# Side jobs of a streaming encoder's input projection: roots in a row, rotated rows further apart, decay later, last part split later

## The chip, the cores and the metric

The kernel runs on one core of one Trainium2 chip. The metric is the device time of one execution in microseconds (us); lower is better. The engines of a core are TensorE (PE, with its weight loads shown as PEld), VectorE (DVE), ScalarE (ACT), GpSimd (POOL) and SyncE (SP), which only issues DMAs here; POOL issues some DMAs too.

## What is computed

One step of a one-layer encoder: a normed input is projected into [z | xBC | dt | q | k | v | gates], then come a state-space scan, differential attention, a mix and a convolutional FFN. 1024 prompt rows and 64 sample rows are treated together, 1088 columns in all. What matters here:

```python
xn = _rmsnorm(x, p['norm_mix_w'])
proj = xn @ p['w_in']
z, xbc, dt_raw, q, k, v, gate_ssm, gate_att = jnp.split(proj, ...)
...
dt = jax.nn.softplus(dt_raw + p['ssm_dt_bias'])          # the decay's steps
acum = jnp.cumsum(dtc * a_neg, axis=1)                   # per chunk, in the scan
...
y_ssm = y_ssm * jax.nn.silu(z)
...
q = _partial_rope(_rmsnorm(q.reshape(b, t, 16, 64), p['q_norm_w']), q_pos)
k = _partial_rope(_rmsnorm(k.reshape(b, t, 16, 64), p['k_norm_w']), q_pos)
k_all = jnp.concatenate([k_past, k], axis=1)             # the cached keys
```

So q and k need, beside their product, a reciprocal root over each head's 64 squares, a weight, and a rotation of the first 16 of 64 dimensions (with the layout used here, those are the first two of eight tiles of 128 rows). All is 32-bit: a float32 operand is split into a high part and a low part (the difference), and a product is three matmuls: high by high, high by low, low by high.

## The kernel before, in words

The stage in question projects q (4 pairs of tiles), k (4 pairs) and z (8 pairs), in this order, 16 pairs numbered 0 to 15 (`INPUT`). One pair is a 2 by 2 block product done with seven products instead of eight (`in_pair`): seven combinations of the weight's quadrants (on the left) times seven combinations of the normed input (on the right: b11, t2, b21, t3, t1, t4, b22), each in two halves of 272 columns. That makes 14 steps per pair, each 12 matmuls of 272 columns, numbered `at` = 0 to 13. The products gather in PSUM banks in piles: pile a holds products 0 and 2, pile b 1 and 3, pile c 4 and 6, pile d 5. A pile that is read midway (a after product 0, b after product 1, c after product 4) is read first and then added to. Piles a are read by ACT (`S.copy`, L677 and L687; the latest is kept in `seen["copy"]`), the others by DVE (L679, L681, L689; `seen["read"]`). There are seven banks in turn, and each pair takes eight.

A finished quarter of the pair goes to `done` one step later (L653): for q and k its squares (L665, L668) are summed into `squares[kind]`, for z it gets a Silu (L658); then it is stored to DRAM (L670). The row buffers `fx` (four), `fc` (three), `fp` (three), `fu` and `ss` (two) are shared by everything in this stage.

The left combinations of the next pair are made beside (`lefts_at`): loads by SP, sums by POOL (L555 to L561), a cast on ACT and a subtraction on DVE for the split (L411, L412). The right parts t3, t1, t4 and b22 had been stored to DRAM and are loaded and split (L411, L412) during pair 0 (`LATER`). The right part b12, for the gates that follow, takes t2's place once product 1 of the last pair has used it: before, load and split are both written at step (1, 1) of pair 15, `at` = 3.

Beside all this run **side jobs**, one turn per product, from the second half of pair 1 on (`take_turn`, L777). A generator in `beside` yields either a number (turns to wait before its next step) or a job (which takes its own turns; the next one comes three turns later, plus what the generator then yields). They are, in this order:

1. `steps` (L694): the decay. Softplus of dt as a series (15 DVE instructions over 288 columns, the tiles `st`, `dt`, `dtt`), cumulative sums by small matmuls, exponentials, and three pieces of decays stored to `a_sc`. Its work tile `four` is one of the two `ss` rows; the other is q's squares, and k's squares take the decay's place.
2. `cached_keys` (L864): eight jobs, each a load of 256 KB by POOL, a cast on ACT, a subtraction on DVE, and two stores.
3. `finishing("q")`, then `finishing("k")` (L796), appended when pair 3 is done. For each: sums of squares over a head (a matmul with `blk`, three pieces of 384, 384 and 320 columns), the root of each (`rstd_of`, L242: Ln, Exp and Square on ACT, two DVE instructions), then twelve jobs for the rows that aren't rotated (`part`) and four for those that are (`turned`, each 272 columns). A `turned` job loads two tiles of rows and the cosines and sines by POOL (L834, L835), and does two scalings (L842), four instructions of rotation (L846 to L849), a cast to the high part and a subtraction to the low (L768, L772), and two stores; for k also a store of the result.

The kernel is written in a framework that orders the instructions of each engine by priority (the order of writing) and by simulated readiness of the operands. `with tc.issue_after(x)` pins what is written inside behind x on x's own engine; `after("copy", "read")` pins behind the latest copy and the latest read. An activation table is loaded in front of an ACT function that the table in force does not hold; `preload_act_table_set(LN_EXP)` loads by hand the one that holds both Ln and Exp.

Of the kernel before, what the change touches and what calls it, by code (L numbers as in the profile page):

```python
# [11 lines left out]
AF = mybir.ActivationFunctionType  # L12
# [11 lines left out]
WIDE = ((0, 384), (384, 384), (768, 320))  # L24
# [66 lines left out]
def hybrid_layer(ctx: ExitStack, tc: tile.TileContext, xT, xt, prm, cst, rope, wvd, win, wbs, wba, wout, wup, wdn,  # L91
# [59 lines left out]
    def weights(block, k, m, pool=None):  # L151
# [4 lines left out]
            V.tensor_tensor(out=lo, in0=w, in1=hi, op=ALU.subtract)  # L156
        return hi, lo

    def product(ps, terms):
        n = len(terms)  # L160
        for i, (a_hi, a_lo, b_hi, b_lo) in enumerate(terms):
            PE.matmul(ps, a_hi, b_hi, start=i == 0, stop=False)  # L162
            PE.matmul(ps, a_hi, b_lo, start=False, stop=False)  # L163
            PE.matmul(ps, a_lo, b_hi, start=False, stop=i == n - 1)  # L164
# [77 lines left out]
    def rstd_of(pool, out, mean, w, tag, scale=1.0, top=384, t=None):  # L242

        t = t or [pool.tile([P, top], F32, name=f"{tag}{i}", tag=f"{tag}{i}") for i in range(2)]
        u, r = (x[: out.shape[0], :w] for x in t)
        act(u, mean, AF.Ln, bias=eps_t[: out.shape[0]], scale=scale)
        act(r, u, AF.Exp, scale=-0.5)
        act(u, r, AF.Square, scale=math.sqrt(0.5 * scale))
        V.scalar_tensor_tensor(u, mean, EPS / scale, u, ALU.add, ALU.mult)
        V.scalar_tensor_tensor(out, u, -1.5, r, ALU.add, ALU.mult)  # L250

# [216 lines left out]
    def row(tag, name, dt=F32):  # L468
        if tag in ("fa", "fs", "fu"):
            w = {"fa": KT * P, "fs": 4 * P, "fu": HT}[tag]  # L470
            return rows_l.tile([P, w], dt, name=name, tag=tag, bufs=IN_ROWS[tag])
        w = {"ss": T}.get(tag, HT)
        return rows_r.tile([P, w], dt, name=name, tag=tag, bufs=IN_ROWS[tag])
# [124 lines left out]
    FIRST_BLOCK = dict(q=B_Q, k=B_K, z=B_Z)  # L598
    LATER = {1: "t1", 3: "t4", 4: "b22"}
    squares, begun_squares = {}, set()  # L600
    seen = {}

    def blocks_of(n):
        kind, j = INPUT[n]
# [9 lines left out]
    def load_part(n, at=None):  # L614
        for s in range(2):
            hi, lo = parts[n, s] = units_of(n, s, at)
            seen["part"] = load(out=lo.bitcast(F32), in_=p_sc[n].rearrange("(k p) t -> p k t", p=P)[:, :, cols(s)])
# [11 lines left out]
    def in_pair(n):  # L629

        kind, j = INPUT[n]
        u1, u2 = row("fx" if n == 1 else "fu", "u1"), row("fu", "u2")
        banks, out = {}, {}

        def pile(key, p, s, start):
            if start:
                banks[key, s] = acc(W2[s])
            ps, w, b = banks[key, s], left[n][p], parts[PARTS[p], s]
            for k in range(4):
                c = slice(P * k, P * (k + 1))  # L640
                for i, (x, y) in enumerate(((0, 0), (0, 1), (1, 0))):
                    seen["mm"] = PE.matmul(ps, w[x][:, c], b[y][:, k], start=start and k == i == 0, stop=k == 3 and i == 2,
                                           skip_group_check=not start)
            return ps

        def to(r, c, s):

            if (r, c) not in out:
                out[r, c] = row("fp", "pre")
            a, w = O2[s], W2[s]  # L650
            return out[r, c][:, a : a + w]

        def done(r, c):  # L653
            cs = slice(HT * c, HT * (c + 1))
            t = out[r, c][:, :HT]
            f = 2 * j + r
            if kind == "z":
                act(t, t, AF.Silu)  # L658
            else:
                if kind not in squares:  # L660
                    squares[kind] = row("ss", "ss")
                ss = squares[kind][:, cs]
                if (kind, c) not in begun_squares:
                    begun_squares.add((kind, c))
                    act(ss, t, AF.Square)  # L665
                else:
                    sq = row("fc", "sq")[:, :HT]
                    act(sq, t, AF.Square)  # L668
                    V.tensor_tensor(out=ss, in0=ss, in1=sq, op=ALU.add)
            load(out={"z": z_sc, "q": q_r, "k": k_r}[kind][P * f : P * (f + 1), cs], in_=t)  # L670

        at = yield
        for _ in range(14):
            p, s = at
            us = cols(s)
            if p == 0:
                seen["copy"] = S.copy(u1[:, us], pile("a", p, s, True))  # L677
            elif p == 1:
                seen["read"] = V.tensor_tensor(out=u2[:, us], in0=pile("b", p, s, True), in1=u1[:, us], op=ALU.add)  # L679
            elif p == 3:  # L680
                seen["read"] = V.tensor_tensor(out=u1[:, us], in0=pile("b", p, s, False), in1=u1[:, us], op=ALU.add)  # L681
            else:
                r, c, key, start, u = {2: (0, 0, "a", False, None), 4: (1, 1, "c", True, u1), 5: (1, 0, "d", True, u1),
                                       6: (0, 1, "c", False, u2)}[p]
                ps = pile(key, p, s, start)
                if u is None:
                    seen["copy"] = S.copy(to(r, c, s), ps)  # L687
                else:
                    seen["read"] = V.tensor_tensor(out=to(r, c, s), in0=ps, in1=u[:, us], op=ALU.add)  # L689
                if s == 1:  # L690
                    ripe.append(lambda r=r, c=c: done(r, c))
            at = yield
# [50 lines left out]
            yield  # L743

    def one_by_one(gen):
        for _ in gen:
            yield 2

    def after(*names):
        pins = ExitStack()  # L750
        for n in names:
            pins.enter_context(tc.issue_after(seen[n].ins))
        return pins

    def job(fetch, scale, hi_of, hi_rows, lo_rows, keep=None):

# [15 lines left out]
            V.tensor_tensor(out=x.bitcast(R32), in0=x, in1=hi, op=ALU.subtract)  # L772
        load(out=lo_rows, in_=x)

    running, clock = [], [0, 0]

    def take_turn():  # L777
        for x in list(running):
            x[0] -= 1
            if x[0] <= 0:  # L780
                x[0] = next(x[1], None)
                if x[0] is None:
                    running.remove(x)
        clock[0] += 1
        if clock[0] >= clock[1]:
            new = next(beside, None)
            if new is None:
                return bool(running)
            if isinstance(new, int):
                clock[1] = clock[0] + new  # L790
            else:
                running.append([next(new), new])
                clock[1] = clock[0] + 3
        return True

    def finishing(kind):  # L796

        d, to, keep, wcol = {"q": (q_r, q_st, None, lambda j: wq8[:, j : j + 1]),
                             "k": (k_r, k_st, kT, lambda j: col(O_KN + j))}[kind]
        if kind == "q":  # L800
            yield 8
        rs = squares[kind]
        for c, w in WIDE:
            ps = stat(w)
            with tc.issue_after(seen["mm"].ins):
                PE.matmul(ps, blk, rs[:, c : c + w], start=True, stop=True)
            t = [row("fx", "n1") for _ in range(2)]
            S.copy(rs[:, c : c + w], ps)
            rstd_of(None, rs[:, c : c + w], rs[:, c : c + w], w, "qn", 1.0 / 64, t=t)
            yield 3  # L810

        def rows_at(y, r0, j, n, c, w):
            return y[r0 + P * j : r0 + P * (j + n), c : c + w].rearrange("(j p) t -> p j t", p=P)
# [45 lines left out]
            yield 1  # L859
        for c in range(0, T, QW):  # L860
            yield turned(c)
            yield 1

    def cached_keys():  # L864
        def part(j):
            def fetch():
                x = row("fx", "x")[:, :PAST]
                G.dma_start(out=x, in_=ckT[P * j : P * (j + 1), :])
                return x

            return job(fetch, None, lambda: row("fc", "xh", R32)[:, :PAST], *(c_st[D * u + P * j : D * u + P * (j + 1), :] for u in range(2)))

        for j in range(KT):
            yield part(j)
# [28 lines left out]
    for at, (p, s) in enumerate(rest):  # L903
# [7 lines left out]
                load_part("b22")  # L911
        if s == 1 and p in LATER:
            split_part(LATER[p], seen["copy"], seen["read"])
    beside = chain(one_by_one(steps()), cached_keys())
    for n in range(1, len(INPUT)):
        blocks = blocks_of(n + 1) if n + 1 < len(INPUT) else None
        u = pairs[1] if n == 1 else begun_in(n)
        for at, (p, s) in enumerate(rest if n == 1 else [(p, s) for p in range(7) for s in range(2)]):
            old, ripe = ripe, []
            u.send((p, s))  # L920
            for x in old:
                x()
            if n == 2 and at in (0, 1):
                make_left(2, 2 + at, blocks)
            lefts_at(n, at, blocks, short={3: "load", 7: 0, 9: 1} if n == 1 else None)
            take_turn()
            if n + 1 == len(INPUT) and (p, s) == (1, 1):
                load_part("b12")
                split_part("b12", seen["copy"], seen["read"])
        del left[n]  # L930
        if n == Q_DONE:
            beside = chain(beside, finishing("q"), finishing("k"))
# [1024 lines left out]
```

## Time and profile before

| | us |
|---|---|
| runs of the kernel before: median (lowest to highest of 3) | 2438.24 (2435.74 to 2441.54) |
| the profiled execution | 2441.61 |
| its span | 2439.8 |
| PE busy | 2393.0 (98%) |
| DVE busy | 1719.7 (70%) |
| ACT busy | 1222.0 (50%) |
| POOL busy | 690.9 (28%) |

The span is that of the instructions; the execution's own time has 1.8 us more around it. Busy shares are means over stages with different limits. In a timeline row the first number is the start in us from the span's start, the second the length, and the bracket at the end holds the engine's idle time just before the row and what ended it. A wait for several things is put down to the one that came last by the profile. A row "x12" is a run of 12 instructions merged.

### The profile page before, as it was taken

How to read it: one execution, taken by the hardware profiler on the slowest of the kernel's cores; microseconds unless marked ns; L12 is line 12 of the kernel's file. 1: busy time of each engine (PE TensorE's matmuls, PEld its weight loads, DVE VectorE, ACT ScalarE, POOL GpSimd, SP SyncE). 2: the span in 40 equal slices, each digit the busy share in tenths (PEclk: the TensorE clock that was granted, in tenths of full speed). 3: DMA queues.
4: the chain of work that ended last, by engine and by line, in shares of the span. 5: the costliest groups of instructions: out<-in, count | busy, mean ns of one | idle time of the engine just before them, and what ended most of it. 6: DMA issues, size and time to landing. Idle time of an engine off the chain costs nothing.

```text
span 2439.8 us, 49478 instructions
## 1 busy us (share of the span) xinstructions
PE 2393.0 (98%) x18744; PEld 2320.5 (95%) x18744; DVE 1719.7 (70%) x3090; ACT 1222.0 (50%) x2689; POOL 690.9 (28%) x757
## 2 busy tenths in 40 slices
PE   8999999999999999999999999999999999999998
PEld 8989989999999999998899999999999999999998
DVE  4676877658687786876678665756866756767765
ACT  6345465356565565657655463434533333353442
POOL 0032333201011010114344332013255554543344
PEclk9999999999999999999999999999999999999999
DMA  7855768675544444337797955764124424357976
GB/s 243 276 178 184 233 212 296 212 208 149 159 154 140 131 146 147 108 120 227 251 337 257 319 180 162 220 210 159 56 85 144 158 96 157 126 185 209 253 181 105
DMA packets 296241, 449.80 MB, mean 184 GB/s; under 512 B 36729, under 2 KB 192514, under 8 KB 296002
## 3 DMA queue, kind: packets, MB, share of 16 engines
q1 hardware_dynamic: 284962, 420.31, 52.3%
q0 software_dynamic: 11040, 26.34, 5.4%
q8 instruction: 147, 2.41, 0.4%
q14 instruction: 92, 0.75, 0.1%
HBM read 294.03 MB, written 152.50 MB: 183 GB/s over the span
## 4 chain that ended last, share of the span: by engine, by line
PE 47%; DVE 4%; DMA 2%; issue 2%; ACT 1%; POOL 0%; SPq 0%; POOLq 0%; DVEq 0%; ACTq 0%
PE mx L1599 13%; PE mx L1773 6%; PE mm L1599 5%; PE mm L162 3%; PE mm L164 3%; PE mm L163 3%; PE mx L162 3%; PE mx L164 3%; PE mx L163 3%; PE mm L1773 2%; PE yi L1288 1%; PE ye L1294 1%; PE stp L1300 1%; PE tr L1267 1%; DMA w_f<-in_wout_dram 1%
## 5 line engine op out<-in xcount | busy, mean ns | idle before, releaser
L162 PE MATMUL mm<-b,w_hi 128*128 128x272 f32 x1576 | 465.8, 296 | 0.0
L164 PE MATMUL mm<-b,w_lo 128*128 128x272 f32 x1576 | 459.3, 292 | 0.0
L163 PE MATMUL mm<-b,w_hi 128*128 128x272 f32 x1576 | 457.9, 291 | 0.0
L162 PEld LDWEIGHTS mm<-b,w_hi 128*128 128x128 f32 x1576 | 296.9, 188 | 6.2 <-issue 5.1
L163 PEld LDWEIGHTS mm<-b,w_hi 128*128 128x128 f32 x1576 | 297.1, 189 | 2.9 <-issue 2.1
L164 PEld LDWEIGHTS mm<-b,w_lo 128*128 128x128 f32 x1576 | 296.5, 188 | 0.7 <-issue 0.2
L983 DVE SCALAR_TENSOR_TENSOR cc<-pre,par,cc 128x272 f32<-128x272 f32 (+1 forms) x288 | 140.2, 491 | 15.9 <-ACT cc L981 13.0
L1599 PE MATMUL mx<-n,wh 128*128 128x272 f32 x1080 | 145.0, 290 | 1.9 <-DVE u L1626 1.0
L1599 PE MATMUL mx<-m,w_hi 128*128 128x272 f32 x752 | 144.6, 289 | 1.1 <-ACT m L411 1.1
L1599 PEld LDWEIGHTS mx<-n,wh 128*128 128x128 f32 x1080 | 139.8, 190 | 2.3 <-DVE u L1626 1.2
L971 POOL COPY pre<-pre 128x3 f32<-128x3 f32 x72 | 22.5, 312 | 417.4 <-DVE cc L985 196.3
L412 DVE TENSOR_TENSOR wh<-w_f,wh 128x512 fp32r<-128x512 f32 (+1 forms) x144 | 139.2, 967 | 1.0 <-ACT wh L411 0.9
L162 PE MATMUL mx<-b,w_hi 128*128 128x272 f32 x472 | 138.7, 294 | 0.5 <-ACT grs L1325 0.5
L164 PE MATMUL mx<-b,w_lo 128*128 128x272 f32 x472 | 137.7, 293 | 1.0 <-DVE w_lo L156 1.0
L156 DVE TENSOR_TENSOR w_lo<-w_f,w_hi 128x1024 fp32r<-128x1024 f32 (+1 forms) x82 | 102.2, 1248 | 51.3 <-ACT w_hi L155 50.3
L1107 ACT ACTIVATE p_t<-sc,mx 128x512 f32<-128x512 f32 (+6 forms) x144 | 106.1, 739 | 64.5 <-DVE mx L1098 30.3
L163 PE MATMUL mx<-b,w_hi 128*128 128x272 f32 x472 | 135.8, 288 | 0.0
L155 ACT CAST w_hi<-w_f 128x1024 fp32r<-128x1024 f32 (+1 forms) x82 | 85.8, 1048 | 71.6 <-PE mm L163 48.7
L1599 PEld LDWEIGHTS mx<-m,w_hi 128*128 128x128 f32 x752 | 118.1, 188 | 1.3 <-ACT m L411 1.3
L1608 ACT ACTIVATE cc<-pre,par 128x544 f32<-128x544 f32 (+1 forms) x44 | 37.2, 846 | 146.7 <-DVE pre L1643 146.6
L1599 PE MATMUL mx<-m,w_lo 128*128 128x272 f32 x376 | 108.3, 289 | 0.0
L1616 POOL TENSOR_TENSOR hb<-hb,cc 128x544 f32<-128x544 f32 (+2 forms) x63 | 67.0, 1078 | 132.6 <-DVE hb L1637 98.5
(461 smaller groups left out, 7084.1 us busy)
## 6 DMA issues: line engine op xcount, KB each, us to landing
w_f<-in_win_dram SPq DMA_DIRECT2D x48, 512.0 KB, 3.9
w_f<-in_wup_dram SPq DMA_DIRECT2D x80, 256.0 KB, 2.6
bc<-a_sc SPq DMA_DIRECT2D x32, 512.0 KB, 5.7
w_f<-in_win_dram SPq DMA_DIRECT2D x60, 256.0 KB, 4.0
b<-y_sc SPq DMA_DIRECT2D x24, 544.0 KB, 8.4
h_sc<-hb SPq DMA_DIRECT2D x44, 272.0 KB, 2.1
ht<-h_sc SPq DMA_DIRECT2D x22, 544.0 KB, 4.7
t_sc<-ht SPq DMA_DIRECT2D x22, 544.0 KB, 2.9
```

The source lines that it names most:

```text
L155: S.copy(hi, w)
L156: V.tensor_tensor(out=lo, in0=w, in1=hi, op=ALU.subtract)
L162: PE.matmul(ps, a_hi, b_hi, start=i == 0, stop=False)
L163: PE.matmul(ps, a_hi, b_lo, start=False, stop=False)
L164: PE.matmul(ps, a_lo, b_hi, start=False, stop=i == n - 1)
L412: V.tensor_tensor(out=lo, in0=src, in1=hi, op=ALU.subtract)
L983: V.scalar_tensor_tensor(cc[:, :m], pre[:, i : i + m], cw(i), cc[:, :m], ALU.mult, ALU.add)
L1107: act(p_t[:n, :nk], sc[c][:n, :nk], AF.Exp, bias=mx[:n, c : c + 1], accum_out=dst)
L1599: PE.matmul(ps, w[x][:, c], b[y][:, k], start=start and k == i == 0, stop=k == 3 and i == 2, skip_group_check=not start)
L1608: act(cc[:, :n], pre[h][:, :n], AF.Identity, bias=col(O_FB + f), scale=cw(0))
L1616: (V if f + 1 == FT else G).tensor_tensor(out=hb[h][:, o : o + n], in0=hb[h][:, o : o + n], in1=cc[:, d : d + n], op=ALU.mult)
L1773: PE.matmul(ps, w[y][:, c], b[z][:, k], start=start and k == j == 0, stop=k == n - 1 and j == 2, skip_group_check=not start)
```

## The change

- `rstd_of` remembers its last ACT instruction as `seen["root"]`. In `finishing`, the roots of the three pieces are no longer each done behind its sum of squares: first the three sums and their copies, two turns apart, then, at one place, a table load by hand and the three roots in a row. For k this place waits until the pair's product 6, 7 or 8. The table load is pinned behind the latest copy and the latest Silu, the roots behind the table load, and each Silu of z behind the latest root. q's eight turns of waiting in front are dropped.
- The rotated rows' jobs come five turns apart (three and two) instead of four.
- The decay's job goes behind the cached keys', and all that it issues is pinned behind the latest copy and read.
- The last part, b12, is still loaded at product 3 of the last pair, and split at product 9.

```diff
+    seen = {}
+
+    def after(*names):
+        pins = ExitStack()
+        for n in names:
+            pins.enter_context(tc.issue_after(seen[n].ins))
+        return pins
...
-        act(u, r, AF.Square, scale=math.sqrt(0.5 * scale))
+        seen["root"] = act(u, r, AF.Square, scale=math.sqrt(0.5 * scale))
...
             if kind == "z":
-                act(t, t, AF.Silu)
+                with after("root"):
+                    seen["silu"] = act(t, t, AF.Silu)
...
     def one_by_one(gen):
-        for _ in gen:
+        while True:
+            with after("copy", "read"):
+                if next(gen, 0) == 0:
+                    return
             yield 2
...
-    running, clock = [], [0, 0]
-
-    def take_turn():
+    running, clock = [], [0, 0, 0]
+
+    def take_turn(at=0):
+        clock[2] = at
...
-        if kind == "q":
-            yield 8
         rs = squares[kind]
-        for c, w in WIDE:
+        for (c, w), gap in zip(WIDE, (2, 2, 1)):
             ps = stat(w)
             with tc.issue_after(seen["mm"].ins):
                 PE.matmul(ps, blk, rs[:, c : c + w], start=True, stop=True)
-            t = [row("fx", "n1") for _ in range(2)]
-            S.copy(rs[:, c : c + w], ps)
-            rstd_of(None, rs[:, c : c + w], rs[:, c : c + w], w, "qn", 1.0 / 64, t=t)
-            yield 3
+            with after("copy"):
+                S.copy(rs[:, c : c + w], ps)
+            yield gap
+        while kind == "k" and clock[2] not in (6, 7, 8):
+            yield 1
+        with after("copy", *(["silu"] if "silu" in seen else [])):
+            table = S.preload_act_table_set(LN_EXP)
+        with tc.issue_after(table.ins):
+            for c, w in WIDE:
+                t = [row("fx", "n1") for _ in range(2)]
+                rstd_of(None, rs[:, c : c + w], rs[:, c : c + w], w, "qn", 1.0 / 64, t=t)
+        yield 3
...
         for c in range(0, T, QW):
             yield turned(c)
-            yield 1
+            yield 2
...
-    beside = chain(one_by_one(steps()), cached_keys())
+    beside = chain(cached_keys(), one_by_one(steps()))
...
-            take_turn()
-            if n + 1 == len(INPUT) and (p, s) == (1, 1):
+            take_turn(at)
+            if n + 1 == len(INPUT) and at == 3:
                 load_part("b12")
+            elif n + 1 == len(INPUT) and at == 9:
                 split_part("b12", seen["copy"], seen["read"])
```

More of the change, by code (lines that the diff above doesn't have):

```diff
@@ L600, in hybrid_layer @@
     squares, begun_squares = {}, set()
-    seen = {}
     def blocks_of(n):
@@ L745, in one_by_one @@
     def one_by_one(gen):
-        for _ in gen:
+        while True:
+            with after("copy", "read"):
+                if next(gen, 0) == 0:
+                    return
             yield 2
[L749 to L753, printed above, removed]
     def job(fetch, scale, hi_of, hi_rows, lo_rows, keep=None):
```

## The prediction, made before the changed kernel ran

> **What bounds the kernel now.** I read the page first: span and the engines' busy shares.
>
> ```profile
> span 2439.8 us, 49478 instructions
> PE 2393.0 (98%) x18744; PEld 2320.5 (95%) x18744; DVE 1719.7 (70%) x3090; ACT 1222.0 (50%) x2689; POOL 690.9 (28%) x757
> ```
>
> PE (TensorE) is busy for 2393.0 of 2439.8 us, so nothing that leaves the number of products alone can bring more than the 46.8 us of idle time, plus what a reduced clock costs. The change touches only the input projections of q, k and z, 116 to 487 us. I cut that stage into 10 us windows; columns: length, busy time of PE, PEld, DVE, ACT, POOL, granted clock, DMA share, GB/s. The first row below is an undisturbed window, the others are those with missing PE time or a reduced clock.
>
> ```profile
> 280.00:290.00 10.00, 10.00 (x82) 10.00 (x81) 8.92 (x14) 5.39 (x12) 2.11 (x3) 1.00 0.75 249
> ...
> 120.00:130.00 10.00, 9.33 (x75) 9.10 (x73) 3.88 (x8) 4.63 (x13) 1.31 (x2) 1.00 1.06 337
> 130.00:140.00 10.00, 6.33 (x37) 5.37 (x35) 9.93 (x13) 7.93 (x10) 3.93 (x3) 0.83 0.94 327
> 140.00:150.00 10.00, 8.91 (x56) 8.37 (x57) 10.00 (x13) 3.18 (x5) 2.49 (x2) 0.82 0.07 26
> ...
> 340.00:350.00 10.00, 9.11 (x63) 8.22 (x64) 6.77 (x14) 9.85 (x12) 0.00 (x0) 1.00 0.54 186
> 350.00:360.00 10.00, 5.74 (x42) 5.09 (x41) 4.94 (x9) 9.73 (x16) 2.44 (x3) 1.00 0.44 139
> ...
> 440.00:450.00 10.00, 7.69 (x57) 7.03 (x57) 9.95 (x19) 5.71 (x12) 2.34 (x2) 1.00 0.76 244
> 460.00:470.00 10.00, 9.61 (x64) 9.61 (x65) 7.27 (x14) 4.85 (x10) 1.29 (x1) 0.83 0.68 226
> ```
>
> There are three holes, each with another engine full beside it: DVE (9.93 and 10.00) in the **opening**, 120 to 150; ACT (9.85 and 9.73) at **k's roots**, 340 to 360; DVE (9.95) at **k's rotated rows**, 440 to 465.
>
> What each hole costs I take from the copies of line 677, which read the first product of each pair. Two of them stand one product apart.
>
> ```profile
> 118.05 0.39 ACT L677 COPY u<-mx 128x272 f32<-128x272 f32 x1
> ...
> 171.07 0.39 ACT L677 COPY u<-mx 128x272 f32<-128x272 f32 x1 [0.26 <-PE mx L642]
> ...
> 302.58 0.39 ACT L677 COPY u<-mx 128x272 f32<-128x272 f32 x1 [3.08 <-PE mx L642]
> ...
> 375.31 0.39 ACT L677 COPY u<-mx 128x272 f32<-128x272 f32 x1 [0.32 <-PE mx L642]
> ...
> 396.46 0.39 ACT L677 COPY u<-mm 128x272 f32<-128x272 f32 x1 [0.32 <-PE mm L642]
> 397.97 0.39 ACT L677 COPY u<-mm 128x272 f32<-128x272 f32 x1
> 417.62 0.39 ACT L677 COPY u<-mm 128x272 f32<-128x272 f32 x1 [0.32 <-PE mm L642]
> ...
> 466.74 0.39 ACT L677 COPY u<-mx 128x272 f32<-128x272 f32 x1 [0.32 <-PE mx L642]
> ```
>
> A product is 397.97 - 396.46 = 1.51 us and a clean pair of 14 is 417.62 - 396.46 = 21.16. The opening runs 28 products from 118.05 to 171.07: 53.0 for 42.3, 10.7 lost. From 302.58 to 375.31 are three pairs: 72.7 for 63.5, 9.2 lost. From 417.62 to 466.74 are two: 49.1 for 42.3, 6.8 lost. Those 26.7 us are all that the change can touch.
>
> **Opening: decay's job goes behind the cached keys' (L914), pinned behind the latest copy and read (L746).** DVE there, first the decay's instructions alone (windows by the tile they share), then one group of them, then two rows of DVE's order:
>
> ```profile
> 120.00:160.00 40.00, 0.00 (x0) 0.00 (x0) 10.14 (x15) 1.04 (x3) 0.91 0.63 211
> ```
>
> ```profile
> L707 DVE SCALAR_TENSOR_TENSOR st<-st,dt 128x288 f32<-128x288 f32 x7 | 5.3, 759 | 0.0
> ```
>
> ```profile
> 137.53 2.37 DVE L412 TENSOR_TENSOR t<-t,t 128x1088 fp32r<-128x1088 f32 x1
> 139.82 1.53 DVE L707 SCALAR_TENSOR_TENSOR st<-st,dt 128x288 f32<-128x288 f32 x1
> ```
>
> and PE's two kinds of waits in it:
>
> ```profile
> 134.03 0.39 PE L642 MATMUL mx<-t,wh 128*128 128x272 f32 x1 [1.48 <-DVE st L707]
> ...
> 139.96 2.86 PE L642 MATMUL mm<-t,wh 128*128 128x272 f32 x11 [0.80 <-DVE t L412]
> ```
>
> PE waits for the low parts of t3, t1 and t4 (L412), and the decay's 15 instructions, 10.14 us, stand between them. Taken out, the second low part of t3 ends near 137 instead of 139.9, and each later one gains as much. Of the 10.7 lost, some 1.2 is work that only moves (the decay's own small matmuls), 3.5 is clock (10 x 0.17 + 10 x 0.18 in the two windows), 6.0 is waiting. What I expect to stay is the 1.48 us at 134.03 (ACT's cast behind a copy, put down to L707), about 2 us where DVE's low parts alone set the pace, and one of the two clock dips, 1.7. Bounds: 0 (casts set it) to -9.5; I take 9.5 - 1.5 - 2 - 1.7, rounded up: **-4.5**.
>
> The moved steps: the eight cached keys start 16 turns earlier. Each is one load, a cast, a subtraction and two stores; the first two loads were issued at 126 in any case, so about one load of 256 KB more comes into the full DMA windows (337 GB/s there): 0.8 us, hidden while t4 and b22, which it delays, are split last; 0.8 if that lead is gone. The decay lands in pair 3 and the start of pair 4, some 190 to 220 us:
>
> ```profile
> 190.00:220.00 30.00, 30.00 (x241) 30.00 (x240) 23.65 (x39) 15.09 (x29) 9.25 (x9) 1.00 0.75 249
> ```
>
> DVE has 6.35 free of 30, some 4 more where five cached subtractions leave, and gets about 11. It is late by a burst of 3.5 us at most, and the next read that PE needs (a pile is added to four products after its first read) has 6 us. It is PE-idle in full above that. Bounds for both together 0 to +4; **+0.7**, near the clean window (8.92 of 10 busy, no PE time missing).
>
> **Roots: three in a row under one table (L807 to L810).** ACT in this stage, by groups (count, busy, mean ns):
>
> ```profile
> L658 ACT ACT_TABLE_LOAD x4 | 5.1, 1283 | 0.1
> L246 ACT ACT_TABLE_LOAD x3 | 3.8, 1283 | 0.1
> L247 ACT ACT_TABLE_LOAD x3 | 3.8, 1283 | 0.1
> L246 ACT ACTIVATE n<-ss,eps_t 128x384 f32<-128x384 f32 (+1 forms) x6 | 3.6, 599 | 0.1
> L248 ACT ACTIVATE n<-n 128x384 f32<-128x384 f32 (+1 forms) x6 | 3.0, 507 | 0.2
> L247 ACT ACTIVATE n<-n 128x384 f32<-128x384 f32 (+1 forms) x6 | 3.0, 504 | 0.1
> ```
>
> ```profile
> 356.61 1.77 PE L642 MATMUL mx<-b,wh 128*128 128x272 f32 x12 [2.49 <-ACT u L677]
> 359.68 1.77 PE L642 MATMUL mx<-b,wh 128*128 128x272 f32 x12 [1.30 <-ACT u L677]
> ```
>
> Today every root of k loads a table for Ln and another for Exp, and a Silu between them loads its own: nine of the ten loads stand at k's roots, 11.5 us, and the copies that PE waits for queue behind them. After: one load in front, nine activations (half of 3.6 + 3.0 + 3.0 = 4.8 us), one load back for the Silu. Seven loads fewer there are 9.0 us of ACT out of some 25 full ones. The block is 1.3 + 4.8 + 1.3 = 7.4 us. Counting the generators' turns, k's roots come at product 7 of pair 9; the next copy that PE can be held by is needed 11 products later, 16.6 us. Behind the block queue three Silus, some five casts and two copies of 0.4 to 0.7 us: 6 us more, 13.4 of 16.6. The Silus, now pinned behind the last root (L658), hold back nothing but z's stores; the next pair reuses such a row buffer only at its product 4. Of the 9.2 lost, 2.2 to 2.7 are the three sums of squares on PE, which stay. Bounds 0 to -7; I take **-5.0**, nearly all, since the two long waits are ACT's and ACT gets below full. For q there is one load more (1.28 us) and a block of 6.1 us in a gap of the same length: 0 to +1.5, **+0.3**.
>
> The Trainium skill (ScalarE: Activation LUTs, What ACT_TABLE_LOAD costs) gives a switch as 1283 ns of load plus 1380 ns of drain, about 2.66 us. The rows here show the first figure, and the Ln's starts follow the load's end at once, so the drain isn't seen in them. By the page the block would be an estimated 10.2 us and the sum still -5.0, with no margin left.
>
> **Rotated rows: five products apart instead of four (L862).** One job is seven DVE instructions: two scalings, the two multiplications that stand first below (8 jobs each), a difference, a sum and the low part. Then the rows that show the trouble:
>
> ```profile
> L847 DVE TENSOR_TENSOR x<-x,rp 128x544 f32<-128x544 f32 x8 | 7.8, 974 | 0.1
> L846 DVE TENSOR_TENSOR rt<-x,rp 128x544 f32<-128x544 f32 x8 | 6.5, 818 | 7.6 <-issue 7.5
> ```
>
> ```profile
> 439.57 0.73 DVE L846 TENSOR_TENSOR rt<-x,rp 128x544 f32<-128x544 f32 x1 [3.46 <-issue]
> ...
> 455.80 1.52 DVE L846 TENSOR_TENSOR rt<-x,rp 128x544 f32<-128x544 f32 x1 [3.02 <-issue]
> ```
>
> ```profile
> 451.01 0.72 POOL L835 DMA_DIRECT2D rp<-in_rope_dram  x1 [5.68 <-DVE u L679]
> ```
>
> The multiplications are (7.8 + 6.5) / 8 = 1.8 us a job; with five more of about half to full that length I estimate 4.8. DVE stands twice, for 3.46 and 3.02 us, before a job's first multiplication: the cosines have not landed. Their load at 451.01 had itself waited 5.68 us at the head of POOL's queue for a buffer (three of its kind, two held by each job), and POOL's sums for the next weights queue behind it. A k job holds its turned rows until turn 9; at four apart the second load after it is due at turn 8, at five at turn 10, so that wait goes. DVE's share falls from 4.8 in 6.05 us to 4.8 in 7.55. The first 3.46 stays: it waits for a load issued into a full DMA. Of 6.8 lost, 1.7 is clock (0.83). Bounds +1 (the jobs last 3 turns longer each way) to -6.5; **-4.0**, since one of the two stops and the overload go.
>
> **Last part split later (L929).** ACT waits for the load of b12, but PE has no hole:
>
> ```profile
> ACT b L411 <- DMA b<-p_b: 5.5, 2, 3.8
> ...
> 470.00:480.00 10.00, 10.00 (x81) 10.00 (x81) 4.87 (x8) 3.43 (x5) 0.00 (x0) 1.00 0.64 206
> ```
>
> The load stays at product 3 of the last pair and the split moves to product 9; its first use is four products of the pair and two of the gates later, 9 us, against 2.2 us of casts and 2.6 of subtractions. **0**; if its cover is gone, +2.
>
> **Sum:** -4.5 + 0.7 - 5.0 + 0.3 - 4.0 = -12.5. The profiled execution took 2441.61 us (span 2439.8 and 1.8 around it), so 2429.1; against the median of the runs, 2438.24, I predict **2425.7**.
>
> **Rivals.** (1) The opening is paced by ACT's casts and DVE's own low parts, not by the decay: the 1.48 us in front of 134.03 speaks for it, the 10.14 us between the low parts against. Then -0.5 instead of -4.5: 2429.7. Chance 0.08. (2) The clock dips stay. The windows at 0.83 hold no single wait of 2 us, and 350 to 360, with 4.26 us missing, has 1.00, so waiting alone doesn't set it. Then 3.5 and 1.7 are not in reach, of which my terms hold about half, 2.6: 2428.3. Chance 0.10. Beside it, the Trainium skill (TensorE: Matmul & The Clock Gate, Part 1: The HAM clock gate) lets the clock fall after an idle window of about 3.4 us; by that rule no hole here would lower it, and the two rows at 0.83 and 0.82 disagree. (3) The pressure only moves: DVE in pair 3 (about 30 of 30 us by the count above) and ACT behind the block make new holes of 3 to 4 us each, with a dip of 1.7 us, and eat most: about -2, 2436. For it: DVE at 8.9 of 10 even in clean windows. Against it: clean at 8.9. Chance 0.15. (4) Slower: third buffer row. The decay's work tile and k's squares share two row buffers with q's; k's first square (pair 4, product 6) must wait until the decay's last matmul (product 0) has read it. Should DVE's backlog in pair 3 exceed these six products, 9 us, ACT would stop there, and with it each copy and weight cast: a backlog of 18 us, the 10.14 and what it delays, costs 9 us and the weights' casts behind it about as much again; with the gains cut to half, 2438.2 + 18 - 6 = 2450. Chance 0.11. My forecast has 0.56.
>
> The changed program is also ordered anew, which I allow 3 us either way. About 0.2%, 4.9 us, is what a measurement of this kernel tells from no change: faster than 2433.4 take the forecast, (1) and (2): 0.74 less 0.02 of their tail; same 0.16; slower 0.12 with (3)'s tail. The range, 2417 to 2440, reaches from -21 (nearly all bounds) over most of case (3).
>
> **What would show it.** Right: no decay instruction before 185 us and PE's loss from 118 to the first copy of pair 2 at 6 us instead of 10.7; two table loads around k's roots, no wait on a copy above 1 us there; no stop of DVE at L846 for the later rows, and pairs 13 to 15 within 3 us of 42.3. Wrong: new PE waits at 190 to 225 us, ACT idle at a Ln for a buffer of its row, or a first square of k that waits for PE.

## The result and the profile after

The kernel after takes **2430.02 us** (median of 9 runs, 2425.79 to 2433.65) against 2439.28 for the kernel before (9 runs beside it); the ratio is **0.9967, 95% interval 0.9958 to 0.9976**: some 8 us, 0.33%, faster (the two medians lie 9.3 us apart). The forecast was 2425.7 with a range of 2417 to 2440. The profiled execution took 2433.65 us, the slowest of the nine. The page's first lines:

```profile
span 2431.9 us, 49445 instructions
...
PE 2390.7 (98%) x18744; PEld 2317.6 (95%) x18744; DVE 1716.9 (71%) x3090; ACT 1213.1 (50%) x2683; POOL 692.3 (28%) x757
```

The span is 7.9 us shorter, and PE's busy time hardly moves. In the new file the lines stand 5 to 12 further down: the first copy of a pair is L685 (was 677), the matmul L649 (642), DVE's reads L687, L689 and L697 (679, 681, 689), the low part L777 (772), the first multiplication of a rotation L858 (846), a split's cast and subtraction L419 and L420 (411 and 412).

The prediction measured stretches by the copies that read the first product of a pair. Before, these copies come 1.7 to 1.8 us behind the pair's first matmul at pairs 2, 8, 11, 13 and 15. After, that mark doesn't hold. At pair 8 TensorE starts at 297.78 us, but the copy stands on ACT behind a square that waits for DVE, and comes 4.8 us behind the matmul:

```profile
302.00 0.66 ACT L676 ACTIVATE sq<-pre 128x544 f32<-128x544 f32 x1 [1.20 <-DVE pre L697]
302.56 0.37 ACT L685 COPY u<-mx 128x272 f32<-128x272 f32 x1
```

So the stretches are taken here from TensorE's own rows. These are the first matmuls of pairs 2, 8, 9, 11, 13 and 15 after, and that of pair 9 before:

```profile
163.68 0.67 PE L649 MATMUL mx<-b,wh 128*128 128x272 f32 x4
...
297.78 3.17 PE L649 MATMUL mx<-b,wh 128*128 128x272 f32 x24
...
322.27 3.18 PE L649 MATMUL mx<-b,wh 128*128 128x272 f32 x24
...
367.08 1.67 PE L649 MATMUL mx<-b,wh 128*128 128x272 f32 x12
...
411.03 1.66 PE L649 MATMUL mm<-b,wh 128*128 128x272 f32 x12
...
459.37 3.18 PE L649 MATMUL mx<-b,wh 128*128 128x272 f32 x24
```

```profile
322.03 3.17 PE L642 MATMUL mx<-b,wh 128*128 128x272 f32 x24
```

Set against before, with the two edits that will matter most beside it (one alone put into the kernel before); a pair without a loss takes 21.15:

| stretch by TensorE's starts, us | before | after | change | five apart alone | roots alone |
|---|---|---|---|---|---|
| opening, pair 0 to pair 2 | 52.9 | 47.9 | -5.0 | 53.3 | 53.7 |
| pairs 2 to 7 (decay's new place, q's roots and plain rows) | 131.6 | 134.1 | +2.5 | 131.6 | 131.6 |
| pair 8 (q's rotated rows) | 21.2 | 24.5 | **+3.3** | 21.2 | 25.9 |
| pairs 9 and 10 (k's roots) | 51.6 | 44.8 | -6.8 | 47.0 | 44.9 |
| pairs 11 and 12 (k's plain rows) | 42.3 | 44.0 | +1.7 | 42.3 | 42.3 |
| pairs 13 and 14 (k's rotated rows) | 49.1 | 48.3 | -0.8 | 43.5 | 45.0 |

The table's changes sum to -5.1. Of the span's 7.9 us, 0.6 more lie ahead of it and 2.2 behind the first score matmul (at 493.09 before and 487.41 after), where no line was changed; in a second profile of the kernel after, that last part took 3.0 us longer. By the copies, from which some numbers of the expectations below come, the opening gained 4.6 us, pairs 8 to 10 gained 5.3 and pairs 13 and 14 gained 1.4. The windows of 10 us after (columns as before):

```profile
120.00:130.00 10.00, 9.74 (x77) 9.52 (x76) 2.67 (x5) 3.12 (x8) 1.83 (x3) 1.00 1.07 350
130.00:140.00 10.00, 8.40 (x63) 7.80 (x61) 8.41 (x9) 8.74 (x11) 4.28 (x3) 1.00 0.92 326
140.00:150.00 10.00, 8.60 (x60) 7.56 (x60) 10.00 (x12) 4.93 (x8) 4.27 (x2) 1.00 0.14 54
...
210.00:220.00 10.00, 10.00 (x75) 9.44 (x76) 6.08 (x11) 4.87 (x10) 5.08 (x4) 1.00 0.39 136
...
300.00:310.00 10.00, 7.65 (x61) 7.43 (x60) 8.43 (x15) 5.11 (x11) 3.38 (x4) 1.00 0.79 277
...
340.00:350.00 10.00, 10.00 (x82) 10.00 (x81) 7.04 (x15) 9.24 (x18) 3.06 (x5) 1.00 0.39 139
350.00:360.00 10.00, 10.00 (x82) 10.00 (x81) 5.50 (x12) 4.53 (x10) 0.75 (x2) 1.00 0.80 265
...
420.00:430.00 10.00, 8.44 (x68) 8.23 (x67) 7.34 (x14) 2.30 (x5) 3.66 (x4) 1.00 0.88 302
430.00:440.00 10.00, 7.60 (x49) 7.38 (x48) 8.20 (x16) 3.62 (x6) 3.54 (x4) 0.83 0.65 207
```

Read it beside the table of before. The opening is at full clock, and PE is busy 26.74 of 30 us instead of 24.57. The hole at k's roots is gone: PE is full at 340 to 360 while ACT is at 9.24. But there are **new holes** at 300 and at 420 to 440. PE's rows there, from its timeline, name what it waited for:

```profile
309.37 3.29 PE L649 MATMUL mx<-t,wh 128*128 128x272 f32 x24 [2.35 <-DVE u L687]
...
377.66 1.78 PE L649 MATMUL mm<-t,wh 128*128 128x272 f32 x12 [1.35 <-DVE u L687]
...
421.82 3.29 PE L649 MATMUL mx<-t,wh 128*128 128x272 f32 x24 [1.56 <-DVE u L687]
...
433.54 0.60 PE L649 MATMUL mx<-b,w_hi 128*128 128x272 f32 x2 [2.40 <-DVE pre L697]
```

Each waits for a read of a pile by DVE that comes late. DVE wasn't out of time (8.43 and 7.34 of 10). The hole at 309 lies at q's rotated rows. There POOL's load of such rows stood 8.95 us, and POOL's sum for the next weights behind it; the cast on ACT waited for the sum, and the weights' low part and then the pile's read at 308.88 came behind that cast on DVE (a multiplication of q's rows that had stood 1.5 us for a store ended at the same time):

```profile
305.74 0.72 POOL L846 DMA_DIRECT2D x<-q_r  x1 [8.95 <-DVE w_lo L420]
306.48 1.28 POOL L565 TENSOR_TENSOR w_f<-w_f,ws 128x512 f32<-128x512 f32 x1
```

```profile
307.80 0.62 ACT L419 CAST w_hi<-w_f 128x512 fp32r<-128x512 f32 x1 [3.54 <-POOL w_f L565]
```

In the second profile of this kernel the same load stood 9.19 us, and the wait is put down to a store of q's low part: a row buffer was still being read. For the other holes, what DVE stood for is in the view of waits (total us, times, longest), 105 to 490 us:

```profile
DVE x L777 <- DMA out_dram<-x: 18.2, 8, 4.5
...
DVE rt L858 <- DMA q_st<-xh: 1.5, 1, 1.5
DVE rt L858 <- DMA rp<-in_rope_dram: 1.2, 1, 1.2
```

Before, the two entries that answer to these were:

```profile
DVE rt L846 <- issue: 7.5, 3, 3.5
...
DVE x L772 <- DMA out_dram<-x: 1.4, 3, 0.7
```

So the stop for the cosines went, as forecast, and **another stop, over ten times what it had been, took its place**: k's low part (L777) is written over the scaled row while the store of k's result (L769) still has to read that row. One case on DVE, and the issue of that row's store by SP:

```profile
408.72 1.11 DVE L834 SCALAR_TENSOR_TENSOR x<-x,par,ss 128x544 f32<-128x544 f32 x1
...
417.32 1.61 DVE L777 TENSOR_TENSOR x<-x,xh 128x544 fp32r<-128x544 f32 x1 [3.18 <-DMA out_dram<-x]
```

```profile
410.48 0.32 SPq L774 DMA_DIRECT2D k_st<-xh  x1
...
412.42 1.25 SPq L769 DMA_DIRECT2D out_dram<-x  x1
```

The row was scaled by 409.8. SP issued its store at 412.42, behind other transfers in its queue; DVE came to the low part and stood 3.18 us, and the pile's read that is queued behind it came late for the product at 421.82. The hole at 433 has less of it: only 0.71 us of the stop stands just ahead, and two rotation instructions at 429.50 and 430.94 took 1.52 and 1.50 us beside POOL's sums, where one like them takes 0.42 at 421.69. Before, DVE met the same wait three times for 1.4 us in all.

### The profile page after: what moved, and what is told of

Same layout as the page of the kernel before. It is cut to its first block, busy times and chain, and to the rows that moved or that the text cites. A ratio compares the mean times of both kernels' runs of the same rounds, so it can differ in the third digit from the quotient of the medians.

```text
span 2431.9 us, 49445 instructions
## 1 busy us (share of the span) xinstructions
PE 2390.7 (98%) x18744; PEld 2317.6 (95%) x18744; DVE 1716.9 (71%) x3090; ACT 1213.1 (50%) x2683; POOL 692.3 (28%) x757
## 5 line engine op out<-in xcount | busy, mean ns | idle before, releaser
L420 DVE TENSOR_TENSOR wh<-w_f,wh 128x512 fp32r<-128x512 f32 (+1 forms) x144 | 136.7, 950 | 0.7 <-ACT wh L419 0.7
L563 POOL TENSOR_TENSOR ws<-w_f 128x512 f32<-128x512 f32 (+1 forms) x47 | 63.1, 1342 | 176.4 <-DMA w_f<-in_wdn_dram 61.7
```

Of the source, the lines that this page charges most:

```text
L420: V.tensor_tensor(out=lo, in0=src, in1=hi, op=ALU.subtract)
L563: G.tensor_tensor(out=s1, in0=q21, in1=q22, op=ALU.add)
```

## The experiments

All times are ratios to the kernel before, run beside each on the same chip (medians 2440.66 us, 2441.04 and 2440.88 for the three groups of four). "After" was 0.9967 and, once more with the last group, 0.9978; differences under 0.001 are not read.

**One part of the change undone at a time.** Roots as before:

```diff
-        with after("copy", *(["silu"] if "silu" in seen else [])):
-            table = S.preload_act_table_set(LN_EXP)
-        ...roots of three pieces in a row
+            rstd_of(None, rs[:, c : c + w], rs[:, c : c + w], w, "qn", 1.0 / 64, t=t)
+            yield 3
```

> The changed kernel with the roots done as before: each behind its own sum of squares, no table load by hand, Silus not pinned, q's eight turns of waiting back. My theory (three separate holes, two of which the change closes): the three pairs around k's roots cost 5.3 us more again, so about 5 us over the changed kernel, 2435. Rival (the changed kernel gains as a whole, because its whole order was made anew, not by part): within 2 us of the changed kernel, or another hole in another place.

Measured: **0.9954 (0.9942 to 0.9967)**, 2427.89 us. My theory of then failed: without the roots in a row the kernel isn't slower. Its first matmuls of pairs 9, 11, 13 and 15:

```profile
319.49 3.17 PE L649 MATMUL mx<-b,wh 128*128 128x272 f32 x24
...
366.91 1.68 PE L649 MATMUL mx<-b,wh 128*128 128x272 f32 x12
...
409.24 1.67 PE L649 MATMUL mm<-b,wh 128*128 128x272 f32 x12
...
451.54 3.17 PE L649 MATMUL mx<-b,wh 128*128 128x272 f32 x24
```

Pairs 9 and 10 take 47.4 us, 4.2 less than before, with eight of the nine table loads at k's roots still in place; k's rotated rows take 42.3, which is clean, and DVE's stop for k's store is 5.1 us. The roots' hole had mostly been closed by something else, and the new roots bring something that costs it back.

Four apart again:

```diff
-            yield 2
+            yield 1
```

> The changed kernel with the rotated rows' jobs four turns apart again. Theory now, after the changed kernel's trace: DVE stands in front of these jobs for DMAs to land (loads of rows and cosines, and k's store that must have read the rows before their low part is written over them), and the spacing only moves that; k's stretch gained 1.4 us, q's stretch has new holes of 2.7 us: so within 2 us of the changed kernel, 2428 to 2432. Rival (the prediction's step: the spacing is worth 4 us): 2434.

Measured: 0.9965 (0.9951 to 0.9978), as expected. With the roots in a row in place, the spacing no longer shows in the time.

Decay first again, not pinned:

```diff
-    beside = chain(cached_keys(), one_by_one(steps()))
+    beside = chain(one_by_one(steps()), cached_keys())
```

> The changed kernel with the decay's job in front of the cached keys' again, and not pinned. Theory (the decay's instructions stand between the low parts of t3, t1 and t4 on DVE): the opening costs 4.6 us more again, so about 2434.5, and the decay's holes at 203 and 209 us (0.9 us) go. Rival (the opening is paced by ACT's casts and DVE's low parts): within 1.5 us of the changed kernel.

Measured: 0.9974 (0.9965 to 0.9982). The opening's loss is back (pair 0 to pair 2: 52.0 us), as the theory had it, but the whole is only 0.0007 above the kernel after, inside the uncertainty.

Last part split at product 3 again:

```diff
-            elif n + 1 == len(INPUT) and at == 9:
                 split_part("b12", seen["copy"], seen["read"])
```

> The changed kernel with b12 split at product 3 of the last pair, right behind its load. Theory: PE has no hole there in either kernel, so no change within 1.5 us of 2430. Rival (ACT's wait for the load holds copies behind it): up to 3 us slower.

Measured: 0.9976 (0.9967 to 0.9985). No difference that can be told; at most 0.001 worse.

**The new stop.** By now the theory was that the new roots bring q's and k's rows into another place of the pair, where the low part meets a store that hasn't been done. Two ways to take the stop away, without touching the roots: the low part of k's rows two products later, or all of k's row jobs three products later.

```diff
-        yield 2 if keep is None else 4
+        yield 2 if keep is None else 6
```

> The changed kernel with k's low part two turns later: six turns behind its high part instead of four, nothing else. Theory (in the changed kernel DVE stands 18.2 us in 8 waits because the low part is written over rows that the store of k has yet to read, and these waits make PE's holes at 377, 421 and 433 us): DVE's waits for that store fall below 5 us, the holes go, 2425 to 2427. Rival (PE's holes there come from DVE's load, not its waits): the waits fall and the time stays within 1.5 us of the changed kernel's 0.9967 of before.

```diff
-        yield 3
+        yield 3 if kind == "q" else 6
```

> The changed kernel with k's row jobs three turns later (six turns behind the roots instead of three), so that they stand at the same products of a pair as with the old roots; the roots and all else as changed. Theory (with the new roots the row jobs fell into a phase in which the low part comes before k's store has landed; the phase is what ate the roots' gain): DVE's waits for the store as in the run with the old roots, 5 us or less, and 2424 to 2426. Rival (the block of roots itself costs elsewhere): unchanged within 1.5 us.

Measured: low part later **0.9951 (0.9938 to 0.9965)**, 2429.93 us; rows later 0.9957 (0.9945 to 0.997). The wait in the first:

```profile
DVE x L777 <- DMA out_dram<-x: 0.5, 1, 0.5
```

18.2 us have become 0.5 (4.1 in the second), and behind pair 2 PE has no hole over 0.3 us in either before the projections end. Pairs 11 and 12 take 42.3 us in both, pairs 13 and 14 take 42.5 and 42.6. That the stop makes the holes at k's rows is shown by this. That the later low part is worth 0.0016 to 0.0027 of the time is a difference of medians; its interval overlaps the first one of the kernel after and lies below the second. Both times are above the forecasts (2425 to 2427, 2424 to 2426).

The hole at 309 is gone in these two as well, but not by the edits: they touch k's rows only, which come behind it. Up to there DVE, ACT, POOL and SP have the same order of instructions in the kernel after, these two, the split at product 3, and two runs further down (both cures, and the kernel after once more). Pair 8 took 24.5 us in the first, 21.5, 21.5 and 21.6 in the next three, 24.9 and 24.8 in the last two. So whether this hole opens differs between executions of one order, and some 3 us between two profiles come from it alone. In the four profiles without the new roots (before, roots as before, five apart alone, decay alone) it is not there.

**One part alone, put into the kernel before.** Five apart:

```diff
-            yield 1
+            yield 2
```

> The kernel before with the rotated rows' jobs five turns apart, nothing else. Theory (spacing alone is worth what the prediction said where the jobs' phase is the old one): about 4 us under before, ratio 0.998 to 0.999. Rival (spacing is worth nothing by itself): within 0.0007 of 1.

Measured: **0.9963 (0.9951 to 0.9975)**: this one line alone is worth as much as the whole change, twice what I expected. Its first matmuls of pairs 9, 11, 13 and 15, and its wait for the cosines:

```profile
321.37 3.18 PE L642 MATMUL mx<-b,wh 128*128 128x272 f32 x24
...
368.39 1.66 PE L642 MATMUL mx<-b,wh 128*128 128x272 f32 x12
...
410.69 1.66 PE L642 MATMUL mm<-b,wh 128*128 128x272 f32 x12
...
454.15 3.18 PE L642 MATMUL mx<-b,wh 128*128 128x272 f32 x24
```

```profile
DVE rt L846 <- issue: 2.1, 1, 2.1
```

Pairs 13 and 14 gain 5.7 us (49.1 to 43.5); the stops for the cosines fall from 7.5 us to 2.1, while those for k's store rise from 1.4 to 7.4. And pairs 9 and 10, where **no line of the roots was changed**, gain 4.6 (51.6 to 47.0). In this trace k's first table load for Ln comes 21.2 us behind the start of pair 9, against 17.8 before, and eight loads stand there instead of nine.

Roots alone (all edits of `rstd_of`, the Silu and `finishing` ahead of its rows):

> The kernel before with the roots in a row, the table load by hand, the pins on the Silus and the earlier start alone. Theory (the hole at k's roots, some 5 us, closes, and the new phase of the row jobs opens others at k's rows, some 3 to 5 us): within 3 us of before, ratio 0.9985 to 1.0005. Rival (the roots are worth 5 us net): ratio 0.998 or less.

Measured: 0.9981 (0.9972 to 0.9989), just under the theory's range. Pairs 9 and 10 gain 6.7, pairs 13 and 14 gain 4.1, pairs 2 to 7 are as before, and pair 8 loses 4.7, with this new wait of PE at q's rotated rows and a clock of 0.83 in the window from 310:

```profile
313.51 0.77 PE L649 MATMUL mx<-t,wh 128*128 128x272 f32 x4 [2.29 <-DVE u L687]
```

Decay behind the cached keys alone (the chain's order and the pins as in the kernel after):

> The kernel before with one edit: decay's job starts behind the cached keys' jobs, as in the kernel after. Theory (the opening's gain is its own and adds to whatever the rest does): the first copy of pair 2 lands near 166 instead of 171 us, 4 to 5 us earlier, and the time falls by 3 to 5 us, ratio 0.998 to 0.9987. Rival (what the opening gains is given back later, because decay then holds TensorE beside the cached queries' pairs and all later row jobs stand in another phase): pair 2 lands near 166 us too, but the first score matmul is within 1.5 us of 493 and the ratio is within 0.0007 of 1.

Measured: 0.9987 (0.9978 to 0.9996), 2437.31 us. The opening takes 48.4 us instead of 52.9, as the theory had it. Pairs 2 to 7 take 134.1 instead of 131.6, as with the whole change, and the first score matmul comes at 493.56, against 493.09 before: the rival's forecast on that place holds in this execution, the theory's on the time, at its upper end. The gain is real but small.

**The last three.** The roots at their new place and in a row, without the table load by hand:

```diff
-            table = S.preload_act_table_set(LN_EXP)
-        with tc.issue_after(table.ins):
             for c, w in WIDE:
```

> The kernel after with the roots at their place and still three in a row, but without the table load put in by hand ahead of them: a block's roots then load tables for Ln and for Exp in turn. Theory (place and number of loads both count): some 6 loads instead of 1 ahead of k's roots, 5 more at 1.28 us, 6.4 us more of ScalarE between two silus, so that TensorE waits 1 to 3 us for a copy in k's block: ratio 0.0005 to 0.0012 above that of the kernel after. Rival (place alone counts, the loads lie beside matmuls): no wait of TensorE on a copy over 1 us at k's roots, ratio within 0.0005 of the kernel after.

Measured: **0.9991 (0.9982 to 1.0)**, against 0.9978 for the kernel after beside it. Table loads by groups, and PE at k's roots:

```profile
L254 ACT ACT_TABLE_LOAD x3 | 3.8, 1283 | 0.1
L255 ACT ACT_TABLE_LOAD x3 | 3.8, 1283 | 0.1
L666 ACT ACT_TABLE_LOAD x2 | 2.6, 1283 | 0.0
```

```profile
347.17 0.75 PE L649 MATMUL mx<-b,w_hi 128*128 128x272 f32 x2 [2.79 <-DVE pre L697]
```

Pairs 9 and 10 take 48.8 us, 4.0 more than in the kernel after. With the roots as before and all else as changed they took 47.4, so being in a row by itself brings nothing there: the six loads of 1.28 us are the cost, and the one load by hand takes five of them away. What PE waits for is put down to DVE, which was busy for 2.31 of 10 us then; ACT, at 9.84, is what both stood behind.

Both cures of the stop together, and the kernel after once more:

> The kernel after with both edits that took VectorE's waits for k's store away: the rotated rows of k begin three products later, and k's low part comes two products later. Theory (the waits on that store are what is left to gain in this stage): waits under 1 us, no hole of TensorE over 1 us behind pair 2, ratio as low as the lower of the two alone, 0.995 to 0.9957. Rival (the later phase pushes the last rows past the projections' end and costs there what it gains): the stage ends earlier, but the span behind the first score matmul is over 1949 us, and the ratio is 0.9965 or more.

> The kernel after once more, on the chip of these three. Theory (VectorE's stand at k's store is a property of the order): the waits of the low part's rows for the store sum to over 10 us again, with holes of TensorE over 1 us at k's rotated rows; ratio 0.9957 to 0.9977. Rival (the profiled execution, the slowest of its nine, was one in which a transfer happened to land late): under 5 us of such waits and no such hole, at the same ratio.

Measured: 0.9954 (0.9941 to 0.9968) with 1.4 us of the stop left, and 0.9978 (0.9969 to 0.9987) with 16.5 us of it. The stop belongs to the order of the work and not to one execution. The two cures together are no better than either: holes of 1.98 and 2.35 us are left at 308 and 429. The first is the one at q's rotated rows. Ahead of the second DVE stood 2.89 us for a load of k's rows, and two scalings and a multiplication then took 2.61 and 1.70 us (0.92 and 0.73 at the same place in the other run) beside POOL's sums. No version was clearly better than the low part two products later.

## Why the prediction was right, and where it wasn't

The time came out inside the range and on the side forecast, 4.3 us above the forecast. Part of that is luck: 2.2 us of the profile's 7.9 lie where nothing was changed, and the roots brought 2 us more than their term while q's rows cost 3 us and k's rows 5 us against theirs. By the steps of the sum:

- **Opening, -4.5: right, with its cause.** Measured -5.0 here and -4.5 alone; no instruction of the decay is left in 120 to 160. Some 1.2 us of it is the decay's own matmuls, which only moved and which the forecast had left out, so -3.8 and -3.3 compare with -4.5. Of the terms, both clock dips went where I had kept one, and the waits fell by less than I thought. The clock was no term of its own: the kernel before with five apart has one of the two dips (0.83 and 1.00 instead of 0.83 and 0.82), and its opening takes 53.3 us all the same.
- **Moved steps, +0.7 (0 to +4): right.** Pairs 2 to 7 are 2.5 us longer in the whole change and with the decay alone, 1.2 of them those matmuls.
- **Roots in a row, -5.0 (0 to -7) at k: right at its place**, measured -6.8 there, all that was lost but the sums of squares, and the table loads are shown to be the cause. The view of ACT's groups has four loads in this stage, two of them at k's roots:

```profile
L817 ACT ACT_TABLE_LOAD x2 | 2.6, 1283 | 0.0
L666 ACT ACT_TABLE_LOAD x2 | 2.6, 1283 | 0.0
```

```profile
338.93 1.28 ACT L817 ACT_TABLE_LOAD   x1
340.23 0.62 ACT L254 ACTIVATE n<-ss,eps_t 128x384 f32<-128x384 f32 x1
...
345.34 0.47 ACT L256 ACTIVATE n<-n 128x320 f32<-128x320 f32 x1
345.83 1.28 ACT L666 ACT_TABLE_LOAD   x1
```

  The block lasts 8.2 us from load to the end of the load back, against 7.4 worked out. By the figure of the Trainium skill (ScalarE: Activation LUTs, What ACT_TABLE_LOAD costs) a drain of 1380 ns would come with each switch. Here Ln starts 1.30 us after the load does, which lasts 1.28, so no drain shows.
- **q's roots, +0.3 (0 to +1.5): right for the roots, wrong for what stands behind them.** Up to pair 7 they cost nothing: 131.6 us alone as before, 134.1 with the whole change as with the decay alone. But pair 8, where q's rotated rows are, took 3.3 us longer here and 4.7 with the roots alone. I counted table loads and had no term for those rows, which come at another place with eight turns of waiting dropped and the roots moved. The rows at 305.74 and 307.80 show how such a place costs; that it opens in some executions only, the runs above show, and what decides it stays open.
- **Rotated rows, -4.0 (+1 to -6.5): mis-sized, -0.8 in the whole change, -5.7 alone.** The mechanism was right (the stop for the cosines fell from 7.5 us to 1.2), but the stop for k's store took its place: 7.4 us with the spacing alone, 9.5 with the roots alone, 18.2 with both, which cost 1.7 us at pairs 11 and 12 and holes at 421 and 433. So one sign of being right failed: pairs 13 and 14 took 48.3 us and not 42.3 within 3.
- **Split later, 0: nothing shown against it.**
- **The sum failed as a sum.** Alone, decay, roots and spacing bring 0.0013, 0.0019 and 0.0037, together 0.0069 or 17 us; all three, with the split, bring 0.0033 and 0.0022 in the two measurements. Spacing alone takes 4.6 us from the pairs of k's roots, the roots in a row 6.7, both 6.8: **one hole, counted by me to one edit, could be closed by one and for two thirds by the other**. Why the spacing closes it, by shifting k's roots in the pair or by what it keeps off ACT, wasn't tried.

Of the rivals, the one that came nearest in mechanism is the third, pressure that only moves: it named DVE, new holes with a dip, and 2436. Its places, pair 3 and ACT behind the roots, were wrong: the new holes stand at the rotated rows. The first (casts pace the opening) and the second (dips stay) fell: that stretch gained 5.0 us and is at full clock. The fourth, k's first square behind the decay, didn't happen: PE is full from 210 to 220.

## What to carry to other kernels

Where several engines are near full, an edit that shifts a job by a few products re-times every queue behind it. Bound that from the waits of rows that are not edited (here an in-place write behind a store that the queue had not yet issued), not only from the cost of what moves. Before adding up gains of several edits, ask of each hole which of them could close it alone, and count it once. Measure a stretch on the engine that bounds it: a copy on ACT that reads TensorE's product came 1.7 us behind the pair's start in one kernel and 4.8 in the next, so a loss read from it lands in the wrong pairs. An in-order engine that overwrites a buffer still to be read by a DMA wants the write put later, or the store earlier in its queue: two products were enough here.

## What the hardware showed unexpectedly

The granted clock doesn't follow the length of a hole alone. After the hole of 2.40 us at 433.54, PE's groups of two matmuls took up to 0.66 us instead of 0.41 until about 437, and the window shows 0.83. After the hole of 2.35 us at 309.37 none did, nor after one of 2.65 us at 310.63 in the second profile of the same kernel, where 24 matmuls took 3.29 us; with both cures the hole there was only 1.98 us, and the 24 behind it took 4.80. The rows behind 433.54:

```profile
434.17 0.66 PE L649 MATMUL mx<-b,w_hi 128*128 128x272 f32 x2
...
438.06 0.29 PE L649 MATMUL mx<-b,w_lo 128*128 128x272 f32 x1
```

The Trainium skill (TensorE: Matmul & The Clock Gate, Part 1: The HAM clock gate) has the clock watched in windows of about 3.4 us that run freely. With half clock for one such window, an estimate by that page, 10 us would show 0.83, as they do here; that a window must be idle as a whole doesn't agree, as no hole of this stage was that long: the longest in any run is 3.05.

DVE's low part took 710 ns at best and 1819 at worst in 11 instructions of one shape. The six that took 1.50 us or more lie beside POOL's sums of weights, the five of 0.71 to 0.73 don't: 1.62 us at 374.43 beside a sum from 374.16, 0.71 at 411.66 with POOL idle. A job's length on DVE thus depends on where it lands, which is one more way in which moved work costs. The Trainium skill (GPSIMD Engine Reference, Specifications) has GpSimd share its SBUF interfaces with VectorE, with contention for instructions that read two inputs from there, as the low part does; the rows agree.
